# Seven products instead of eight for five heads' gate and value, four pairs instead of three in the MLP

## The chip, the cores and the metric

One core of a Trainium2 chip runs the whole program in one launch. The metric is the device time in microseconds of one execution, in the median of several; lower is better.

## The reference, cut to what matters

One layer of a trunk on 256 tokens of width 2048, in float32: a retention mixer with 8 heads, then a squared-ReLU MLP of width 8192, each behind an RMSNorm and added to its input, and a last RMSNorm.

```
h = rmsnorm(x, norm1)
q, k, v, g = split(h @ w_in, [2048, 4096, 8192])   # w_in 2048 x 12288; per head q,k 256, v,g 512 columns
q, k = rotary(q), rotary(k) * DK**-0.5
o = ((q @ k.T) * decay) @ v                         # chunk-causal, per head
o = head_norm(o) * silu(g)
x = x + o @ w_out                                   # 4096 x 2048
h = rmsnorm(x, norm2)
x = x + square(relu(h @ w_up)) @ w_down             # 2048 x 8192, 8192 x 2048
return rmsnorm(x, final_norm)
```

## The kernel before, in words

All weights are read once from HBM, 1 MB at a time, by DMAs that SyncE's queue issues in order. Every float32 operand is split in two float32r parts, a high one (a cast, on ScalarE) and a low one (operand minus high, on VectorE), and a product is three matmuls: high by high, high by low, low by high (lines 87 and 88, where the first two share one matmul of 512 columns, lines 102 to 106, and line 153). `load_block` loads a block of 128 x 2048 weights in `raw` (3 buffers) and splits it in two pairs `wh`, `wl` of 128 x 1024 (4 buffers of each); a buffer is free again once TensorE has read it for the last time.

The 128-row slices of the inner dimension are called kt; T = 256 tokens are NB = 2 row halves b. `proj_cols` makes queries and keys and the MLP's first product (weights stationary, tokens moving), `proj_rows` makes gates, values and the output product (tokens stationary, 512 weight columns moving): for each kt, each b and each 512 columns, three matmuls. A head h runs `gates`, `gate_silu`, `queries`, `values`; the rest of the previous head is put in between as fillers after a block: `mix(h-1)` in the gates, `turn(h-1)` (transposes of the result into `ys`) in the queries, `scores(h)` in the values.

The MLP's second product is done four times (q: 2048 of the 8192 rows), each in two halves of 1024 columns, by `seven`. Of the 16 kt of a q, the first 2*SP = 6 are three pairs; a pair of kt, the two row halves and the two column blocks are a 2 x 2 by 2 x 2 block product, done with seven block products instead of eight (Winograd's form of Strassen's scheme), 3 matmuls each and pair. The other 10 kt are done as in `proj_rows`, in 5 blocks (`regular`, r). Four weight blocks b11, b12, b22, b21 are loaded in `sraw`; four sums of them are made in place by VectorE (`plus`, line 196); the sums of the left side are made in `sums` beside the MLP's first product. Products that go to one quarter alone accumulate in its PSUM bank; those that go to several have banks of their own (`chain`, `fifth`) and are added to x by VectorE (`sub_out`, line 580). The order of r and of the seven products is a string: `"rwr13r25r6r74"`, where w is the loading of the four blocks; the last of the eight calls keeps 4 kt to the end (`late=4`) so that the quarters finish one after the other (`finish`).

Each engine works through its instructions in order. That order is set at build time by the Tile framework's list planner: of the instructions that are ready by its own costs it takes the one that is earliest in the program, so work written later can be put ahead of work that waits. All 8 PSUM banks are one rotating pool.

Of the kernel before, what the change touches and what calls it, by code (L numbers as in the profile page):

```python
# [28 lines left out]
SP = 3  # L29
QT = 16  # L30


@with_exitstack
def trunk_kernel(ctx: ExitStack, tc: tile.TileContext, io, out):

# [13 lines left out]
    def bank(name):  # L49
        return ps.tile([P, 512], F32, tag="bank", name=name)  # L50
# [28 lines left out]
    def proj_cols(src, xs, accs, fillers=()):  # L79
        for g in range(KT // 4):  # L80
            parts = load_block(src[g], 4, 512)
            for j, (wh, wl) in enumerate(parts):
                kt = 4 * g + j
                for o, acc in enumerate(accs):
                    c = slice(o * P, (o + 1) * P)
                    both = xs[:, kt].rearrange("p a t -> p (a t)")
                    nc.tensor.matmul(acc, wh[:, c], both, start=(kt == 0), stop=False)  # L87
                    nc.tensor.matmul(acc[:, :T], wl[:, c], xs[:, kt, 0, :], start=False, stop=(kt == KT - 1))  # L88
            for f in [f for at, f in fillers if at == g]:
                f()  # L90
# [3 lines left out]
    def proj_rows(blocks, per, xs, accs, nk, after=(), late=0, done=None, lead=None):  # L94
# [3 lines left out]
        def add(kt, wh, wl, b, cs):  # L98
            t = slice(b * P, (b + 1) * P)
            for c in cs:  # L100
                n = slice(c * 512, (c + 1) * 512)
                nc.tensor.matmul(accs[b][c], xs[:, kt, 0, t], wh[:, n], start=(kt == 0), stop=False)  # L102
                nc.tensor.matmul(accs[b][c], xs[:, kt, 0, t], wl[:, n], start=False, stop=False)  # L103
            for c in cs:
                n = slice(c * 512, (c + 1) * 512)
                nc.tensor.matmul(accs[b][c], xs[:, kt, 1, t], wh[:, n], start=False, stop=(kt == nk - 1))  # L106
# [19 lines left out]


    def seven(quads, blocks, xs, sx, sub_out, done, order, late=0):
        acc = [[bank("acc_d") for _ in range(2)] for _ in range(NB)]
        chain, fifth = bank("acc_s"), bank("acc_5")  # L130
        begun = set()
        raws = []

        def load():
            r = mp.tile([P, SP * 512], F32, tag="sraw", name="sraw", bufs=4)
            nc.sync.dma_start(r, quads[len(raws)])
            raws.append(r)
            return r

        def split(r):  # L140
            parts = []
            for p0 in range(0, SP, 2):
                n = min(2, SP - p0) * 512
# [12 lines left out]
        def product(to, key, r, left):  # L156
            parts = split(r)
            for p, (wh, wl) in enumerate(parts):
# [3 lines left out]
                mm(to, key, xl, wh, p == SP - 1)  # L162

        def part(k, b):
            return lambda p: (xs[:, 2 * p + k, 0, b * P : (b + 1) * P], xs[:, 2 * p + k, 1, b * P : (b + 1) * P])

        def total(i):
            return lambda p: (sx[:, p, i, 0], sx[:, p, i, 1])

        def add(kt, wh, wl, b, cs, last=False):  # L170
            t = slice(b * P, (b + 1) * P)
            for c in cs:
                n = slice(c * 512, (c + 1) * 512)
                mm(acc[b][c], (b, c), xs[:, kt, 0, t], wh[:, n], False)
                mm(acc[b][c], (b, c), xs[:, kt, 0, t], wl[:, n], False)
            for c in cs:
                n = slice(c * 512, (c + 1) * 512)
                mm(acc[b][c], (b, c), xs[:, kt, 1, t], wh[:, n], last)
# [3 lines left out]
        def regular(g):  # L182
            for j, (wh, wl) in enumerate(load_block(blocks[g], 2, 1024)):
                kt = 2 * SP + 2 * g + j
# [5 lines left out]

        def whole():
            for name in ("b11", "b12", "b22", "b21"):
                w[name] = load()

        def plus(to, other):
            nc.vector.tensor_add(w[to], w[to], w[other])

        def p1():
            product(chain, "s", w["b11"], total(0))
            sub_out(0, 0, chain, -1)  # L200

        def p2():
            product(acc[0][0], (0, 0), w["b21"], part(1, 0))

        def p3():
            product(acc[0][1], (0, 1), w["b22"], total(4))

        def p4():
            plus("b21", "b22")
            product(acc[1][0], (1, 0), w["b21"], part(1, 1))  # L210

        def p5():
            plus("b11", "b12")
            product(fifth, "5", w["b11"], total(1))
            sub_out(0, 1, fifth, 1)
            sub_out(1, 1, fifth, 1)
            plus("b12", "b22")

        def p6():
            plus("b22", "b11")  # L220
            product(chain, "s", w["b22"], total(2))
            sub_out(0, 1, chain, 1)

        def p7():
            product(chain, "s", w["b12"], total(3))
            sub_out(1, 0, chain, -1)
            sub_out(1, 1, chain, 1)

        w = {}
        steps = {"w": whole, "1": p1, "2": p2, "3": p3, "4": p4, "5": p5, "6": p6, "7": p7}  # L230
# [12 lines left out]


    xs = cp.tile([P, KT, 2, T], F32R, tag="xs", name="xs")
    xr = cp.tile([P, KT, T], F32, tag="ys", name="xr", padded_shape=[P, VT * 2, T])
# [13 lines left out]
    pw = bank("pw")  # L260
# [14 lines left out]
    with tc.tile_pool(name="ap", bufs=1) as ap:  # L275
# [32 lines left out]
        def first_norm():  # L308
# [6 lines left out]
            psr = bank("psr")  # L315
# [9 lines left out]
        def gates(h, after, lead=None):  # L325
            acc = [[bank("acc_g")] for _ in range(NB)]
            proj_rows(io["w_g"][h], 4, xs, acc, KT, after, lead=lead)
# [9 lines left out]
        def queries(h, fillers):  # L337
            acc = [bank("acc_qk") for _ in range(4)]
            proj_cols(io["w_qk"][h], xs, acc, fillers)
# [18 lines left out]
        def values(h, fillers):  # L358
            acc = [[bank("acc_v")] for _ in range(NB)]
            proj_rows(io["w_v"][h], 4, xs, acc, KT, fillers)  # L360
# [5 lines left out]
        def scores(h):  # L366

            qk = st["qk"]
            pst = bank("pst")
# [16 lines left out]
        def mix(h):  # L386
# [3 lines left out]
            for b in range(NB):  # L390
                po = bank("po")
# [20 lines left out]
        def turn(h):  # L412
            y = st["y"]
            for i in range(2):
                pt = bank("pt")
# [4 lines left out]
                for j in range(2):  # L420
                    k = 4 * h + 2 * i + j
                    split_scaled(ys[:, k], pt[:, j * T : (j + 1) * T], gain[:, k : k + 1])

        for h in range(H):
            if h == 0:
                gates(h, [], lead=lead_x)
                ys = cp.tile([P, VT, 2, T], F32R, tag="ys", name="ys")
# [5 lines left out]
                )  # L433
            else:
                gates(h, [(1, lambda h=h: mix(h - 1))])
                gate_silu()
                queries(h, [(1, lambda h=h: turn(h - 1))])
            if h == 0:
                nc.sync.dma_start(dec, io["dec"])
            values(h, [(1, lambda h=h: scores(h))])  # L440


        acc0 = [[bank("acc_o") for _ in range(2)] for _ in range(NB)]
# [5 lines left out]
    x1s = cp.tile([P, KT, 2, T], F32R, tag="xs", name="x1s")  # L449
# [26 lines left out]
    def turn_x(half):  # L476
        for i in range(4):
            pt = bank("ptx")
# [5 lines left out]
            for j in range(2):  # L484
                split_scaled(x1s[:, k0 + j], pt[:, j * T : (j + 1) * T], norm2[:, k0 + j : k0 + j + 1])
# [7 lines left out]
    acc1 = [[bank("acc_o") for _ in range(2)] for _ in range(NB)]  # L493
# [10 lines left out]
    def second_norm():  # L504
        psr = bank("psr2")
# [8 lines left out]
    big = cp.tile([P, VT * 2 * T], F32R, tag="ys", name="big")  # L514
    hs = big[:, : QT * 2 * T].rearrange("p (k a t) -> p k a t", k=QT, a=2)
    n0 = QT * 2 * T
    sx = big[:, n0 : n0 + SP * 5 * 2 * P].rearrange("p (k s a t) -> p k s a t", k=SP, s=5, a=2)
# [22 lines left out]
    def sums(p, s):  # L540


        a11, a21 = s[:, 0, :P], s[:, 0, P:]
        a12, a22 = s[:, 1, :P], s[:, 1, P:]
        u = mp.tile([P, 4, P], F32, tag="u", name="u")
        nc.vector.tensor_sub(u[:, 0], a21, a22)
        nc.vector.tensor_sub(u[:, 1], a11, u[:, 0])
        nc.vector.tensor_sub(u[:, 2], a21, a11)
        nc.vector.tensor_sub(u[:, 3], a12, u[:, 1])
        nc.scalar.copy(sx[:, p, 1:, 0], u)  # L550
        nc.vector.tensor_sub(sx[:, p, 1:, 1], u, sx[:, p, 1:, 0].bitcast(F32))
        for a in range(2):
            nc.scalar.activation(sx[:, p, 0, a], hs[:, 2 * p, a, :P].bitcast(F32), AF.Copy, scale=-1.0)

    for q in range(4):
        for c in range(4):
            acc = [bank("acc_u") for _ in range(4)]
            proj_cols(io["w_up"][4 * q + c], x1s, acc, [(1, second_norm)] if q == 0 and c == 0 else ())
            for i in range(2):
                s = mp.tile([P, 2, T], F32, tag="s", name="s", bufs=2)  # L560
                for j in range(2):
# [3 lines left out]
                    nc.scalar.copy(s[:, j], acc[o][:, T:])  # L565
                    nc.vector.tensor_add(s[:, j], acc[o][:, :T], s[:, j])
                    nc.vector.scalar_tensor_tensor(t, s[:, j], 0.0, rsrow2, op0=ALU.max, op1=ALU.mult)
                    nc.scalar.activation(s[:, j], t, AF.Square)
                    nc.scalar.copy(hs[:, k, 0], s[:, j])
                    nc.vector.tensor_sub(hs[:, k, 1], s[:, j], hs[:, k, 0].bitcast(F32))  # L570
                if 2 * c + i < SP:
                    sums(2 * c + i, s)
# [3 lines left out]
        for half in range(2):  # L576

            def sub_out(b, c, acc, sign, half=half):
# [5 lines left out]
                io["w_down_s"][q][half], io["w_down_r"][q][half], hs, sx, sub_out,  # L584
# [27 lines left out]

# [47 lines left out]
```

## Time and profile before

| | |
|---|---|
| median of 3 runs | 1473.11 us (1472.92 to 1474.33) |
| the profiled execution | 1472.67 us, its span 1470.5 us |
| TensorE matmul busy | 1453.9 us, 99% of the span, 7096 instructions |
| VectorE busy | 978.7 us, 67% |
| ScalarE busy | 735.3 us, 50% |
| GpSimd busy | 16.3 us, 1% |
| DMA | 280.45 MB, mean 191 GB/s |

The span is what lies between the first and the last instruction of the program in the trace; 2.2 us of the profiled execution lie around it. The duration that a row gives for a matmul is from issue to its modelled end; matmuls overlap, so what one costs is the distance between two starts.

### The profile page before, as it was taken

What the parts mean: (1) busy time and instruction counts of PE and PEld (TensorE: products, weight loads), DVE (VectorE), ACT (ScalarE), POOL (GpSimd) and SP (SyncE); (2) the same over time, 40 slices, a digit from 0 to 9 for tenths busy, and PEclk for the clock granted to TensorE, in tenths of its full rate; (3) what the DMA queues carried; (4) which work ended last, traced back from release to release, by engine and by line L of the source; (5) the groups of instructions that cost most, each with busy time, mean ns of one, the idle gap of its engine ahead of it and who ended that gap; (6) DMA issues with size and microseconds to landing.
All of it is one profiled execution on the core that took longest, in us unless ns stands there. A gap on an engine that the chain in (4) does not pass through costs nothing.

```text
span 1470.5 us, 18118 instructions
## 1 busy us (share of the span) xinstructions
PE 1453.9 (99%) x7096; PEld 1215.9 (83%) x7096; DVE 978.7 (67%) x1305; ACT 735.3 (50%) x994; POOL 16.3 (1%) x28
## 2 busy tenths in 40 slices
PE   9999999999999999999999999999999999999997
PEld 7788888888888888888888888888888888888885
DVE  6556565656565656546466689676897678866787
ACT  7444444444444444434345555465555555556554
POOL 0000000000000000000000000000000000000000
PEclk9999999999999999999999999999999999999999
DMA  9555555545555545765545545655556546565451
GB/s 349 210 186 181 174 175 191 176 172 174 191 177 175 176 174 194 268 239 180 197 170 177 198 153 185 240 197 175 177 187 234 179 165 209 192 215 186 172 200 58
DMA packets 43989, 280.45 MB, mean 191 GB/s; under 512 B 5248, under 2 KB 6144, under 8 KB 14208
## 3 DMA queue, kind: packets, MB, share of 16 engines
q1 hardware_dynamic: 43344, 276.15, 53.5%
q0 software_dynamic: 416, 3.15, 0.6%
q8 instruction: 55, 0.90, 0.2%
q14 instruction: 30, 0.25, 0.0%
q10 hardware_dynamic: 144, 0.01, 0.0%
HBM read 277.18 MB, written 2.10 MB: 190 GB/s over the span
## 4 chain that ended last, share of the span: by engine, by line
PE 96%; DVE 1%; ACT 1%; issue 1%; DMA 0%; POOL 0%; SPq 0%; POOLq 0%; ACTq 0%; DVEq 0%
PE acc_d L153 18%; PE acc_u L87 16%; PE acc_qk L87 8%; PE acc_u L88 8%; PE acc_qk L88 4%; PE acc_v L103 4%; PE acc_o L102 4%; PE acc_o L106 4%; PE acc_o L103 4%; PE acc_g L103 4%; PE acc_v L106 4%; PE acc_g L102 4%; PE acc_v L102 4%; PE acc_g L106 4%; PE acc_s L153 3%; PE po L397 1%
## 5 line engine op out<-in xcount | busy, mean ns | idle before, releaser
L65 DVE TENSOR_TENSOR wl<-raw,wh 128x1024 fp32r<-128x1024 f32 x456 | 553.4, 1223 | 429.1 <-ACT wh L64 428.6
L64 ACT CAST wh<-raw 128x1024 fp32r<-128x1024 f32 x456 | 475.2, 1049 | 520.1 <-PE acc_u L87 144.8
L87 PE MATMUL acc_u<-x1s,wh 128*128 128x512 f32 x1024 | 361.3, 397 | 0.0
L88 PE MATMUL acc_u<-x1s,wl 128*128 128x256 f32 x1024 | 286.4, 281 | 0.0
L153 PE MATMUL acc_d<-wh,big 128*128 128x512 f32 x784 | 245.2, 392 | 0.8 <-ACT wh L147 0.5
L87 PEld LDWEIGHTS acc_u<-x1s,wh 128*128 128x128 f32 x1024 | 192.3, 188 | 46.9
L88 PEld LDWEIGHTS acc_u<-x1s,wl 128*128 128x128 f32 x1024 | 191.8, 188 | 0.9 <-DVE wl L65 0.6
L87 PE MATMUL acc_qk<-xs,wh 128*128 128x512 f32 x512 | 181.8, 398 | 0.0
L153 PEld LDWEIGHTS acc_d<-wh,big 128*128 128x128 f32 x784 | 147.2, 188 | 33.9 <-ACT wh L147 0.9
L153 PE MATMUL acc_d<-wl,big 128*128 128x512 f32 x392 | 150.1, 393 | 0.0
L88 PE MATMUL acc_qk<-xs,wl 128*128 128x256 f32 x512 | 143.4, 281 | 0.0
L147 ACT CAST wh<-sraw 128x1024 fp32r<-128x1024 f32 x112 | 90.9, 834 | 104.2 <-PE acc_d L153 91.4
L87 PEld LDWEIGHTS acc_qk<-xs,wh 128*128 128x128 f32 x512 | 96.2, 188 | 23.3
L148 DVE TENSOR_TENSOR wl<-sraw,wh 128x1024 fp32r<-128x1024 f32 x112 | 103.3, 952 | 11.9 <-ACT wh L147 11.3
L103 PE MATMUL acc_v<-wl,xs 128*128 128x512 f32 x256 | 100.8, 394 | 0.7 <-DVE wl L65 0.7
L102 PE MATMUL acc_g<-wh,xs 128*128 128x512 f32 x256 | 100.3, 395 | 1.1 <-ACT wh L72 1.1
L103 PE MATMUL acc_g<-wl,xs 128*128 128x512 f32 x256 | 101.2, 395 | 0.0
L102 PE MATMUL acc_v<-wh,xs 128*128 128x512 f32 x256 | 100.3, 393 | 0.3 <-ACT wh L64 0.3
L102 PE MATMUL acc_o<-wh,ys 128*128 128x512 f32 x256 | 100.5, 392 | 0.0
L106 PE MATMUL acc_v<-wh,xs 128*128 128x512 f32 x256 | 100.1, 391 | 0.0
L103 PE MATMUL acc_o<-wl,ys 128*128 128x512 f32 x256 | 100.1, 391 | 0.0
L106 PE MATMUL acc_g<-wh,xs 128*128 128x512 f32 x256 | 99.7, 389 | 0.0
(114 smaller groups left out, 1507.2 us busy)
## 6 DMA issues: line engine op xcount, KB each, us to landing
raw<-in_w_up SPq DMA_DIRECT2D x64, 1024.0 KB, 4.9
raw<-in_w_down_r SPq DMA_DIRECT2D x40, 1024.0 KB, 4.9
raw<-in_w_qk SPq DMA_DIRECT2D x32, 1024.0 KB, 4.9
raw<-in_w_v SPq DMA_DIRECT2D x32, 1024.0 KB, 4.9
raw<-in_w_o SPq DMA_DIRECT2D x32, 1024.0 KB, 4.9
raw<-in_w_g SPq DMA_DIRECT2D x28, 1024.0 KB, 5.0
sraw<-in_w_down_s SPq DMA_DIRECT2D x32, 768.0 KB, 4.5
raw<-in_w_g SPq DMA_DIRECT2D x16, 256.0 KB, 6.6
```

What stands on the lines that cost most here:

```text
L64: nc.scalar.copy(wh, r)
L65: nc.vector.tensor_sub(wl, r, wh.bitcast(F32))
L87: nc.tensor.matmul(acc, wh[:, c], both, start=(kt == 0), stop=False)
L88: nc.tensor.matmul(acc[:, :T], wl[:, c], xs[:, kt, 0, :], start=False, stop=(kt == KT - 1))
L102: nc.tensor.matmul(accs[b][c], xs[:, kt, 0, t], wh[:, n], start=(kt == 0), stop=False)
L103: nc.tensor.matmul(accs[b][c], xs[:, kt, 0, t], wl[:, n], start=False, stop=False)
L106: nc.tensor.matmul(accs[b][c], xs[:, kt, 1, t], wh[:, n], start=False, stop=(kt == nk - 1))
L147: nc.scalar.copy(wh[:, :n], c)
L148: nc.vector.tensor_sub(wl[:, :n], c, wh[:, :n].bitcast(F32))
L153: nc.tensor.matmul(to, x, w, start=(key not in begun), stop=last, skip_group_check=True)
L397: nc.tensor.matmul(po, s, w, start=(n == 0), stop=(n == len(terms) - 1))
```

## The change

1. `seven` is made general: number of pairs from `sx`, weight buffers handed in (`raws`), the first result for a quarter of the output marked as first. Signs are moved to the left side, so that product 1 takes the plain high and low parts, without a negated copy (lines 552 and 553 go).
2. For heads 1 to 5, `gates`, `gate_silu` and `values` are replaced by `gates_values`: one product of 1024 columns (512 of g, 512 of v) by `seven` with SPR = 3 pairs and 5 regular blocks, order `"rwr1r3s2r56r74"` (s: the scores). Results go to two tiles in SBUF: ScalarE copies the first, VectorE adds the others. `mix(h-1)` and `turn(h-1)` move into the queries. The left sums are made once, in `sums_x`, in head 0's values. Heads 0, 6 and 7 stay as they were, with some fillers moved.
3. The MLP's second product takes SPM = 4 pairs and 4 regular blocks; order `"rw1r32r56r74"`, and `"rw1r3r25647r"` with `late=2` for the last call. Two of the four weight sums, b12 += b22 and b21 += b22, are made there by an accumulating DMA from SBUF to SBUF that GpSimd issues, 1 MB each; the other two stay on VectorE. In the program the sums stand directly behind the product that last needs the old block.
4. The 8 PSUM banks become two pools (sides) of 4. `ys`, `hs` and the raw weight blocks share three tiles of SBUF (ya, yb, yc).

```
-    def bank(name):
-        return ps.tile([P, 512], F32, tag="bank", name=name)
+    def bank(name, side):
+        return ps.tile([P, 512], F32, tag="bank%d" % side, name=name, bufs=4)
...
+        def plus(to, other):
+            if to in by_dma:
+                nc.gpsimd.dma_start(w[to], w[other], accum_op=ALU.add)
+            else:
+                nc.vector.tensor_add(w[to], w[to], w[other])
...
         def p1():
-            product(chain, "s", w["b11"], total(0))
-            sub_out(0, 0, chain, -1)
+            product(chain, "s", w["b11"], part(0, 0))
+            out(0, 0, chain, 1)
+            plus("b11", "b12")
+            plus("b12", "b22")
         def p2():
             product(acc[0][0], (0, 0), w["b21"], part(1, 0))
+            plus("b21", "b22")
         def p3():
-            product(acc[0][1], (0, 1), w["b22"], total(4))
+            product(acc[0][1], (0, 1), w["b22"], total(3))
+            plus("b22", "b11")
         def p4():
-            plus("b21", "b22")
             product(acc[1][0], (1, 0), w["b21"], part(1, 1))
...
+        def gates_values(h):
+            sg = ap.tile([P, NB, DV], F32, tag="sg", name="sg")
+            vf = ap.tile([P, NB, DV], F32, tag="xh", name="vf", bufs=2)
+            v = ap.tile([P, NB, 2, DV], F32R, tag="v", name="v")
+            to = (sg, vf)
+            def sub_out(b, c, bank, sign, first):
+                t = to[c][:, b]
+                if first:
+                    nc.scalar.copy(t, bank)
+                else:
+                    nc.vector.tensor_tensor(t, t, bank, op=ALU.add if sign > 0 else ALU.subtract)
+            def done(acc, b, c):
+                t = to[c][:, b]
+                nc.vector.tensor_add(t, t, acc[b][c])
+                if c == 0:
+                    nc.scalar.activation(t, t, AF.Silu, scale=rs[:, b : b + 1])
+                else:
+                    split_scaled(v[:, b], t, rs[:, b : b + 1])
+            seven(
+                io["w_gv_s"][i], io["w_gv_r"][i], [sraw[:, j] for j in range(4)], x0, st["sx"],
+                sub_out, done, "rwr1r3s2r56r74", 1, extra=lambda: scores(h),
+            )
...
+            elif h in STRASSEN_HEADS:
+                last = h == STRASSEN_HEADS[-1]
+                queries(h, [(1, lambda: mix(h - 1))] + ([] if last else [(3, lambda: turn(h - 1))]))
+                gates_values(h)
...
+                io["w_down_s"][q][half], io["w_down_r"][q][half], [raw3[:, j] for j in range(3)] + [raw1], hs, sx, sub_out,
...
-                "rw13r25r647rr" if last and half == 1 else "rwr13r25r6r74",
-                late=4 if last and half == 1 else 0,
+                "rw1r3r25647r" if last and half == 1 else "rw1r32r56r74",
+                1 - half, late=2 if last and half == 1 else 0, by_dma=("b12", "b21"),
```

## Rows read from the trace of the kernel before

**Rows 1.** The page, part 1: busy time of each engine.

```profile
PE 1453.9 (99%) x7096; PEld 1215.9 (83%) x7096; DVE 978.7 (67%) x1305; ACT 735.3 (50%) x994; POOL 16.3 (1%) x28
```

**Rows 2.** The page, part 4: the chain of waits by engine.

```profile
PE 96%; DVE 1%; ACT 1%; issue 1%; DMA 0%; POOL 0%; SPq 0%; POOLq 0%; ACTq 0%; DVEq 0%
```

**Rows 3.** Waits of whole span: who waited for whom, total, times, longest.

```profile
DVE wl L65 <- ACT wh L64: 428.6, 316, 3.6
ACT wh L64 <- PE acc_u L87: 144.8, 98, 2.9
```

**Rows 4.** Windows: head 1, its queries, the two halves of a second product.

```profile
core 0: us, PE busy (x) PEld busy (x) DVE busy (x) ACT busy (x) POOL busy (x), PEclk, DMA share, GB/s
79.76:150.62 70.86, 70.86 (x346) 59.46 (x345) 41.60 (x57) 32.53 (x40) 1.09 (x2) 1.00 0.51 177
103.84:127.32 23.48, 23.48 (x137) 20.50 (x136) 11.86 (x14) 11.64 (x17) 0.00 (x0) 1.00 0.52 183
1025.26:1067.41 42.15, 42.15 (x186) 34.30 (x185) 36.72 (x45) 24.12 (x34) 0.00 (x0) 1.00 0.50 173
1067.41:1109.56 42.15, 42.15 (x185) 34.21 (x184) 37.15 (x39) 21.51 (x25) 0.00 (x0) 1.00 0.57 199
```

**Rows 5.** Timeline of PE: start, duration, what; ends of two runs of matmuls.

```profile
127.32 0.39 PE L102 MATMUL acc_v<-wh,xs 128*128 128x512 f32 x1
...
138.31 0.81 PE L374 MATMUL pst<-qk 128*128 128x256 f32 x3
...
1025.26 0.39 PE L153 MATMUL acc_d<-wh,big 128*128 128x512 f32 x1
...
1109.56 0.39 PE L87 MATMUL acc_u<-x1s,wh 128*128 128x512 f32 x1
```

**Rows 6.** DVE by line and form in 1025.26 to 1109.56, busy and mean ns.

```profile
L65 DVE TENSOR_TENSOR wl<-raw,wh 128x1024 fp32r<-128x1024 f32 x18 | 21.5, 1221 | 5.5 <-ACT wh L64 5.5
L196 DVE TENSOR_TENSOR sraw<-sraw 128x1536 f32<-128x1536 f32 x8 | 14.1, 1758 | 0.2
L148 DVE TENSOR_TENSOR wl<-sraw,wh 128x512 fp32r<-128x512 f32 x14 | 9.6, 686 | 0.6 <-ACT wh L147 0.4
L580 DVE TENSOR_TENSOR x<-x,acc_s 128x512 f32<-128x512 f32 x8 | 5.3, 682 | 1.4 <-PE acc_s L153 1.4
L570 DVE TENSOR_TENSOR big<-s,big 128x256 fp32r<-128x256 f32 x4 | 1.6, 420 | 0.0
```

**Rows 7.** Timeline of DVE where head 2's queries end.

```profile
188.31 0.87 DVE L271 SCALAR_TENSOR_TENSOR ys<-pt,gain,ys 128x256 fp32r<-128x256 f32 x2
189.34 0.88 DVE L271 SCALAR_TENSOR_TENSOR ys<-pt,gain,ys 128x256 fp32r<-128x256 f32 x2 [0.15 <-ACT ys L270]
...
197.73 0.78 DVE L346 TENSOR_TENSOR sum<-acc_qk,sum 128x256 f32<-128x256 f32 x2
...
203.11 3.49 DVE L65 TENSOR_TENSOR wl<-raw,wh 128x1024 fp32r<-128x1024 f32 x3
```

**Rows 8.** DMA issues: form, count, KB each, median us to landing.

```profile
raw<-in_w_down_r SPq DMA_DIRECT2D x40, 1024.0 KB, 4.9
sraw<-in_w_down_s SPq DMA_DIRECT2D x32, 768.0 KB, 4.5
x<-in_x POOLq DMA_DIRECT2D x1, 2048.0 KB, 14.2
fnorm<-in_final_norm POOLq DMA_DIRECT2D x1, 1024.0 KB, 5.5
```

**Rows 9.** Timeline of DVE: the last quarter's add.

```profile
1461.43 0.68 DVE L456 TENSOR_TENSOR x<-acc_d,x 128x512 f32<-128x512 f32 x1
```

**Rows 10.** Timeline of PE: the last matmul.

```profile
1460.20 0.39 PE L153 MATMUL acc_d<-wh,big 128*128 128x512 f32 x1
```

More of the change, by code (lines that the diff above doesn't have):

```diff
@@ L28 @@
 WARM = 8
-SP = 3
+SPR = 3
+SPM = 4
 QT = 16
+STRASSEN_HEADS = range(1, 6)
 @with_exitstack
@@ L85, in proj_cols @@
                     c = slice(o * P, (o + 1) * P)
-                    both = xs[:, kt].rearrange("p a t -> p (a t)")
+                    both = xs[kt].rearrange("p a t -> p (a t)")
                     nc.tensor.matmul(acc, wh[:, c], both, start=(kt == 0), stop=False)
-                    nc.tensor.matmul(acc[:, :T], wl[:, c], xs[:, kt, 0, :], start=False, stop=(kt == KT - 1))
+                    nc.tensor.matmul(acc[:, :T], wl[:, c], xs[kt][:, 0, :], start=False, stop=(kt == KT - 1))
             for f in [f for at, f in fillers if at == g]:
@@ L124, in proj_rows, with seven @@
                     done(b, c)
-    def seven(quads, blocks, xs, sx, sub_out, done, order, late=0):
-        acc = [[bank("acc_d") for _ in range(2)] for _ in range(NB)]
-        chain, fifth = bank("acc_s"), bank("acc_5")
+    def seven(quads, blocks, raws, xs, sx, sub_out, done, order, side, late=0, extra=None, by_dma=()):
+        np_ = len(sx)
+        acc = [[bank("acc_d", side) for _ in range(2)] for _ in range(NB)]
+        fifth, chain = bank("acc_5", 1 - side), bank("acc_s", 1 - side)
         begun = set()
[L132 to L138, printed above, removed]
+        taken = set()
+        names = ("b11", "b12", "b22", "b21")
+        w = dict(zip(names, raws))
         def split(r):
             parts = []
-            for p0 in range(0, SP, 2):
-                n = min(2, SP - p0) * 512
+            for p0 in range(0, np_, 2):
+                n = min(2, np_ - p0) * 512
                 wh = wp.tile([P, 1024], F32R, tag="wh", name="wh", bufs=4)
@@ L156, in product @@
         def product(to, key, r, left):
-            parts = split(r)
-            for p, (wh, wl) in enumerate(parts):
+            for p, (wh, wl) in enumerate(split(r)):
                 xh, xl = left(p)
@@ L161, in product, with out @@
                 mm(to, key, xh, wl, False)
-                mm(to, key, xl, wh, p == SP - 1)
+                mm(to, key, xl, wh, p == np_ - 1)
         def part(k, b):
-            return lambda p: (xs[:, 2 * p + k, 0, b * P : (b + 1) * P], xs[:, 2 * p + k, 1, b * P : (b + 1) * P])
+            t = slice(b * P, (b + 1) * P)
+            return lambda p: (xs[2 * p + k][:, 0, t], xs[2 * p + k][:, 1, t])
         def total(i):
-            return lambda p: (sx[:, p, i, 0], sx[:, p, i, 1])
+            return lambda p: (sx[p][:, i, 0], sx[p][:, i, 1])
+        def out(b, c, acc, sign):
+            sub_out(b, c, acc, sign, (b, c) not in taken)
+            taken.add((b, c))
         def add(kt, wh, wl, b, cs, last=False):
@@ L189, in regular @@
                         add(kt, wh, wl, b, range(2), kt == QT - 1)
+        def plus(to, other):
[3 more added lines that the diff above has]
+                nc.vector.tensor_add(w[to], w[to], w[other])
         def whole():
[L192 to L196, printed above, removed]
+            for i, name in enumerate(names):
+                nc.sync.dma_start(w[name], quads[i])
         def p1():
-            product(chain, "s", w["b11"], total(0))
-            sub_out(0, 0, chain, -1)
+            product(chain, "s", w["b11"], part(0, 0))
+            out(0, 0, chain, 1)
+            plus("b11", "b12")
+            plus("b12", "b22")
         def p2():
             product(acc[0][0], (0, 0), w["b21"], part(1, 0))
+            plus("b21", "b22")
         def p3():
-            product(acc[0][1], (0, 1), w["b22"], total(4))
+            product(acc[0][1], (0, 1), w["b22"], total(3))
+            plus("b22", "b11")
         def p4():
-            plus("b21", "b22")
             product(acc[1][0], (1, 0), w["b21"], part(1, 1))
         def p5():
[L213 to L217, printed above, removed]
+            product(fifth, "5", w["b11"], total(0))
+            out(0, 1, fifth, 1)
+            out(1, 1, fifth, 1)
         def p6():
-            plus("b22", "b11")
-            product(chain, "s", w["b22"], total(2))
-            sub_out(0, 1, chain, 1)
+            product(chain, "s", w["b22"], total(1))
+            out(0, 1, chain, -1)
         def p7():
[L225 to L230, printed above, removed]
+            product(chain, "s", w["b12"], total(2))
+            out(1, 0, chain, 1)
+            out(1, 1, chain, -1)
+        steps = {"w": whole, "1": p1, "2": p2, "3": p3, "4": p4, "5": p5, "6": p6, "7": p7, "s": extra}
         g = 0
@@ L325, in gates @@
         def gates(h, after, lead=None):
-            acc = [[bank("acc_g")] for _ in range(NB)]
-            proj_rows(io["w_g"][h], 4, xs, acc, KT, after, lead=lead)
+            acc = [[bank("acc_g", 1)] for _ in range(NB)]
+            proj_rows(io["w_g"][h], 4, x0, acc, KT, after, lead=lead)
             st["acc_g"] = acc
@@ L421, in turn, with sums_x @@
                     k = 4 * h + 2 * i + j
-                    split_scaled(ys[:, k], pt[:, j * T : (j + 1) * T], gain[:, k : k + 1])
+                    split_scaled(ys[k], pt[:, j * T : (j + 1) * T], gain[:, k : k + 1])
+        def sums_x():
+            sx3 = ap.tile([P, 4, 2, P], F32R, tag="xh", name="sx3", bufs=2)
+            to = [sxc[:, 0], sxc[:, 1], sx3]
+            for p in range(SPR):
+                for k in (2 * p, 2 * p + 1):
+                    nc.scalar.activation(xr[:, k], xr[:, k], AF.Copy, scale=norm1[:, k : k + 1])
+                k = 2 * SPR + 2 * p
+                u = xr[:, k : k + 2].rearrange("p a (s t) -> p (a s) t", s=2)
+                sums(to[p], (xr[:, 2 * p], xr[:, 2 * p + 1]), u)
+            st["sx"] = to
+        def gates_values(h):
[16 more added lines that the diff above has]
+                    split_scaled(v[:, b], t, rs[:, b : b + 1])
+            i = h - STRASSEN_HEADS[0]
+            seven(
+                io["w_gv_s"][i], io["w_gv_r"][i], [sraw[:, j] for j in range(4)], x0, st["sx"],
+                sub_out, done, "rwr1r3s2r56r74", 1, extra=lambda: scores(h),
+            )
+            st["sg"], st["v"] = sg, v
         for h in range(H):
@@ L433, in trunk_kernel @@
                 )
-            else:
-                gates(h, [(1, lambda h=h: mix(h - 1))])
+                nc.sync.dma_start(dec, io["dec"])
+                values(h, [(1, sums_x), (2, lambda: scores(0))])
+                ys_part("ya", 0, 16)
+            elif h in STRASSEN_HEADS:
+                last = h == STRASSEN_HEADS[-1]
+                queries(h, [(1, lambda: mix(h - 1))] + ([] if last else [(3, lambda: turn(h - 1))]))
+                gates_values(h)
+                if last:
+                    ys_part("yb", 16, 12)
+                    ys_part("yc", 28, 4)
+            else:
+                first = h == STRASSEN_HEADS[-1] + 1
+                gates(h, ([(0, lambda: turn(h - 2))] if first else []) + [(2 if first else 1, lambda: mix(h - 1))])
                 gate_silu()
[L437 to L443, printed above, removed]
+                queries(h, [(1, lambda: turn(h - 1))])
+                values(h, [(1, lambda: scores(h))])
+        acc0 = [[bank("acc_o", 0) for _ in range(2)] for _ in range(NB)]
         proj_rows(io["w_o"][0], 2, ys, acc0, VT, [(1, lambda: mix(H - 1)), (4, lambda: turn(H - 1))])
@@ L492, in trunk_kernel @@
             add_residual(acc0, 0, b, c)
[L493 removed]
+    acc1 = [[bank("acc_o", 1) for _ in range(2)] for _ in range(NB)]
     proj_rows(io["w_o"][1], 2, ys, acc1, VT, [(2, lambda: turn_x(0))])
@@ L538, in finish @@
                 nc.sync.dma_start(out[b * P : (b + 1) * P, n], x[:, b, n])
[L540 to L553, printed above, removed]
     for q in range(4):
         for c in range(4):
-            acc = [bank("acc_u") for _ in range(4)]
+            acc = [bank("acc_u", (c + 1) % 2) for _ in range(4)]
             proj_cols(io["w_up"][4 * q + c], x1s, acc, [(1, second_norm)] if q == 0 and c == 0 else ())
             for i in range(2):
-                s = mp.tile([P, 2, T], F32, tag="s", name="s", bufs=2)
+                s = [mp.tile([P, T], F32, tag="s", name="s", bufs=4) for _ in range(2)]
                 for j in range(2):
@@ L564, in trunk_kernel @@
                     k = 4 * c + o
[L565 to L572, printed above, removed]
+                    nc.scalar.copy(s[j], acc[o][:, T:])
+                    nc.vector.tensor_add(s[j], acc[o][:, :T], s[j])
+                    nc.vector.scalar_tensor_tensor(t, s[j], 0.0, rsrow2, op0=ALU.max, op1=ALU.mult)
+                    nc.scalar.activation(s[j], t, AF.Square)
+                    nc.scalar.copy(hs[k][:, 0], s[j])
+                    nc.vector.tensor_sub(hs[k][:, 1], s[j], hs[k][:, 0].bitcast(F32))
+                if 2 * c + i < SPM:
+                    u = mp.tile([P, 4, P], F32, tag="u", name="u")
+                    sums(sx[2 * c + i], s, u)
         if q == 3:
@@ L576, in trunk_kernel, with sub_out @@
         for half in range(2):
-            def sub_out(b, c, acc, sign, half=half):
+            def sub_out(b, c, acc, sign, first, half=half):
                 n = slice(half * 1024 + c * 512, half * 1024 + (c + 1) * 512)
@@ L610, in _blocks, with _seven_blocks @@
     return np.ascontiguousarray(w).reshape(n // cols, k // (P * rows), P, rows * cols)
+def _seven_blocks(w, pairs):
+    lead = w.shape[:-2]
+    w = w.reshape(-1, QT, P, 1024)
+    s = w[:, : 2 * pairs].reshape(-1, pairs, 2, P, 2, 512).transpose(0, 2, 4, 3, 1, 5)
+    s = np.stack([s[:, i, j] for i, j in ((0, 0), (0, 1), (1, 1), (1, 0))], axis=1)
+    r = w[:, 2 * pairs :].reshape(-1, QT // 2 - pairs, 2, P, 1024).transpose(0, 1, 3, 2, 4)
+    return s.reshape(lead + (4, P, pairs * 512)), r.reshape(lead + (QT // 2 - pairs, P, 2048))
 def kernel(**inputs):
@@ L630, in cols @@
         return np.ascontiguousarray(u.reshape(n, P).T)
+    w_down = a["mlp_w_down"][0].reshape(4, QT * P, 2, 1024).transpose(0, 2, 1, 3)
+    w_down_s, w_down_r = _seven_blocks(w_down, SPM)
+    hs = slice(STRASSEN_HEADS[0], STRASSEN_HEADS[-1] + 1)
+    gv = np.concatenate([u.reshape(D, H, DV)[:, hs].transpose(1, 0, 2) for u in (g, v)], axis=2)
+    w_gv_s, w_gv_r = _seven_blocks(gv, SPR)
     arrays = {
```

79 lines of the change are left out of this document (46 added, 33 removed).

## The prediction, made before the change was run

> **What bounds the kernel now.** First the engines' busy shares: TensorE is busy 99% of the span, VectorE 67%, ScalarE 50% [rows 1]. Then the chain of waits, which says the same of the end: 96% of it is TensorE, and no DMA is in it [rows 2]. Then the waits: ScalarE's casts wait for TensorE to free a `wh` buffer, and VectorE's low parts wait for ScalarE [rows 3]; both are ahead of TensorE and held back by it. So each matmul taken away is worth its distance to the next, as long as VectorE keeps up. The windows show where that is in doubt: VectorE is busy 41.60 of 70.86 us in a head of the old kind, but 36.72 and 37.15 of 42.15 us (88%) in the two halves of a second product, with TensorE still without a gap there [rows 4]. The granted clock is 1.00 in all of them, the 2.4 GHz level, and I leave it there. The profiled execution took 1472.67 us, 0.44 under the median of the runs; I sum against the former and add the 0.44 at the end.
>
> **The price of a matmul** of 512 columns is the distance of starts. In head 1's values 48 matmuls lie between 127.32 and 138.31: 0.2290 us each. In the MLP 366 (two calls of 183) lie between 1025.26 and 1109.56: 0.2303 each [rows 5]. The difference, 0.0013 x 183 = 0.24 us per call, is all that the old `seven` loses to VectorE at 88%.
>
> **TensorE's part.** Gates and values of a head take 2 x 16 kt x 2 b x 3 = 192 matmuls now. By `seven`: 7 products x 3 pairs x 3 = 63, and 10 kt x 2 b x 2 c x 3 = 120, together 183: 9 fewer in each of five heads, 45. The MLP's call goes from 63 + 120 = 183 to 7 x 4 x 3 + 8 x 12 = 180: 3 fewer in eight calls, 24. That is 69 x 0.229 = 15.8 us less, 1456.9 us. The 10.3 us of it in the heads need VectorE to hold a new load there; the 5.5 in the MLP need the transfers to be on time.
>
> **VectorE in heads 1 to 5.** A 1024-column low part costs 3.49 / 3 = 1.16 us when several follow each other [rows 7], a 512-column one 0.69 and a weight sum of 1536 columns 1.76 [rows 6], about 0.08 less in a row. The stretch from the first r to the last product then holds 10 x 1.16 + 7 x (1.16 + 0.61) + 4 x 1.68 = 30.7 us; two `sub_out` and four adds of 0.6 (3.6; the first copy of each quarter goes to ScalarE, which is half idle); queries' sums and rotation, 203.11 - 197.73 = 5.4; turn's four, 1.75 [rows 7]; scores and the splits of v, some 2.6. Together 44.1, against 183 x 0.229 = 41.9 plus 2.0 for scores and transposes on TensorE, 43.9. As about 4 us (last adds, v) fall in the next queries, where VectorE has 11.86 of 23.48 us of work [rows 4] and gets some 3 us of mix as well, the stretch is 40 of 43.9, 91%: just above the 88% that cost 0.24 us.
>
> The tight place is its start. Let t = 0 be the first r matmul; three `wl` buffers are then ready, as now. VectorE does rotation and turn from -1.25 (0.46 us before the queries end plus 0.79 us of transposes) to 5.9, the second r's last part to 7.1, product 1's two to 8.8, then the two sums that the program puts ahead of the third r, b11 and b12, to 12.2, the third r's first part to 13.3. TensorE gets there after 48 matmuls of r and 9 of product 1, at 13.05, and its second matmul, the first that reads the low part, is due at 13.3. So it fits with nothing to spare; afterwards VectorE gains. If the rotation ended later, up to the 3.4 us of the two sums would show. Bounds 0 and 3.4 us per head; I take the 0.24 of the like stretch, 1.2 us in all.
>
> **The MLP's transfers.** Per call VectorE's own sums go from 4 x 1.68 to 2 x 2.26 (1.76 x 2048/1536, less 0.08), its product splits from 7 x 1.77 to 14 x 1.16, its regular splits from 10 x 1.16 to 8 x 1.16: 0.7 us less than before, so its load is no worry. What is new is a wait: b22 += b11 on VectorE may start only when the transfer b12 += b22 has read b22. Queued behind it on VectorE stand low parts of product 2, and TensorE waits for those. Again with t = 0 at the first r: the last evictions of the first product (12 instructions of 0.42 in three lines like L570's [rows 6]) and product 1's second part end at 4.7, b11 += b12 at 6.9; the transfer starts then. TensorE is at product 2's second half after 78 matmuls, 17.86; ahead of that stand the sum (2.26) and a split (1.16), so the transfer must land by 14.4, 7.5 us after its start. The second transfer, b21 += b22, has 19 us (two r and three products) before product 4 and is hidden; in the last call it has only three products, 8.2 us.
>
> No row shows an accumulating transfer. From below: 1 MB by the same queue, GpSimd's, landed in 5.5 us. From above: 2 MB by that queue, under load, in 14.2. The loads give a slope of (4.9 - 4.5) per 256 KB, 1.6 us per MB [rows 8]; if the target has to be read too, 5.5 + 1.6 = 7.1, the nearest that the rows give for one in quiet, and with a load running beside it more. I take 8.0, 0.5 us late, in the seven calls of the common order: 3.5 us. Ends: 0, and 6.7 x 7 = 47.
>
> The Trainium skill ("Collectives: The Full Stack", section on the bandwidth ceiling) bears on this from the other side: an add in the DMA engine needs two source reads on one ring and ran there at half the rate of a copy (ratio 1.93). No row here shows that. By it the 1 MB's own part of the landing would double; an estimate from that page and the load's 4.9 us is 9.8 us (twice 4.9), and the sum would go up by some 13 us, towards the rival of late transfers below.
>
> **What I cost at nothing.** `sums_x` (six scalings on ScalarE, three sets of four short subtractions and one split, 5 us of VectorE) lies in head 0's values, where VectorE has as much room as in other heads; uncovered it is 5 us once. Loads: the bytes are the same, 16 MB of transfers come on top of 280 and the DMA share in the second product is 0.50 to 0.57 [rows 4]; SyncE's queue waits for buffers, not for HBM. The banks: with two sides of four the queries' first four banks need `chain` free, which product 7's two results release while product 4 runs (9 x 0.229 = 2.06 us, the reads 0.68 each [rows 6]); turn's two banks go straight to the quarters, and the planner can put the other row half's matmuls first. Bounds 0 and 1 us per call. The tail: keeping 2 kt instead of 4 spaces the last quarters by 6 x 0.229 = 1.37 instead of 2.75 us. The last add starts now 1461.43 - 1460.43 = 1.0 us after the last matmul is through [rows 9, 10], as it stands behind another quarter's; it could be 2.4. I take no change.
>
> **Sum.** 1472.67 - 15.8 + 1.2 + 3.5 = 1461.6; on the median 1462.
>
> **The rivals.**
> (a) VectorE becomes the bound in the heads. For: 44.1 us of work in a stretch of 43.9, with the two early sums ahead of a split that is due. Against: the old second halves run gapless at 88%, and the planner can move work. Taking 2.2 us in each head, the middle of 1 and 3.4: 11 instead of 1.2, 1472; the heads would gain nothing.
> (b) The transfers land late, the slower side. Place: the eight calls of `seven`, VectorE's queue in front of b22 += b11. Price: (landing - 7.5) in seven calls. It takes back all that was gained from a landing of 9.6 us on (15.8 - 1.2 = 14.6 over seven calls gives 2.1), and is slower by over 3 us from 10.0 on. At 11.5 us: 28 us, 1486. For: a target that must be read, loads in the same engines, and a planner that may put the sum too early in VectorE's queue. Against: 5.5 us for a plain megabyte, and the planner may as well put product 2's parts ahead of the sum, which lengthens the cover to the next r, another 1.4 us.
> (c) The change doesn't do what it says: the split of the banks makes TensorE wait where eight rotating ones did not, some 0.7 us in each of 13 calls, 9 us: 1471.
>
> **How the numbers follow.** The forecast 0.66 (1456 to 1467), (a) 0.12, (b) 0.17, (c) 0.05. Against 1473.1, 0.2% or 3 us is about what a measurement of this kernel can tell from no change. Faster: the forecast and nearly all of (a) and (c) in their lower parts, 0.76; within 3 us: 0.07; slower: (b), 0.17. The low end is the bare matmul count with no new stall, 1456; the high end takes in (a), (c) and of (b) landings up to 10.4 us, 1479.
>
> **What would show it.** 69 fewer matmuls of 512 columns from heads and second product. The distance of starts stays 0.229 to 0.231 in the heads' new stretches and in the MLP's (right), or goes over 0.235 there (a, b). A wait of VectorE's L-line of the weight sums for a DMA, with low parts and then TensorE late behind it, would show (b); in the transfer rows a landing under 8 us would exclude it. Waits of TensorE for reads of banks would show (c). The forecast is wrong if TensorE's gaps in these stretches come to more than 10 us, or if VectorE's work there is above 95% of the time.

## The result and the profile after

The changed kernel takes 1481.34 us (median of 4 runs, 1480.31 to 1482.88), the kernel before 1473.65 on the same chip: ratio 1.0053, 95% interval 1.0036 to 1.0071. It is 0.5% slower, where 1462 was forecast and 1479 was the upper end; rival (b), the late transfers, is what happened.

The page's parts 1 and 4 of the changed kernel, against [rows 1, 2]: TensorE has 69 matmuls less and is busy 4.9 us less, but in a span that is 10.6 us longer; VectorE's share of the chain went from 1 to 5%, a DMA's from 0 to 4%.

```profile
PE 1449.0 (98%) x7027; PEld 1208.2 (82%) x7027; DVE 1056.0 (71%) x1398; ACT 778.2 (53%) x1027; POOL 29.2 (2%) x44
...
PE 88%; DVE 5%; DMA 4%; issue 2%; ACT 1%; SPq 0%; POOLq 0%; POOL 0%; ACTq 0%; DVEq 0%
```

Windows of it (columns as in [rows 4]): head 1, then head 1's seven products alone, then first and second half of the first second product.

```profile
82.14:151.01 68.87, 68.87 (x338) 57.69 (x336) 53.38 (x71) 36.95 (x50) 1.10 (x2) 1.00 0.48 168
...
107.59:151.01 43.42, 43.42 (x195) 35.57 (x193) 38.05 (x50) 24.77 (x35) 0.00 (x0) 1.00 0.47 159
...
841.87:883.41 41.54, 41.54 (x182) 33.75 (x181) 36.74 (x42) 26.09 (x32) 1.75 (x2) 1.00 0.73 226
883.41:931.73 48.32, 43.34 (x182) 34.97 (x181) 36.18 (x35) 23.10 (x22) 1.71 (x2) 0.96 0.70 218
```

The heads did as was forecast: 68.87 us instead of 70.86 [rows 4], no gap, VectorE at 88% of the stretch. So did this first half: 41.54 us (those of the other three q take 41.6 to 42.6). The second half lost almost 7 us, at a lower granted clock. Among the waits of the whole span (who waited for whom, total, times, longest), these lines are new. L204 is the line of `plus` that VectorE does, L153 the low parts of `split`, L158 the matmuls of `seven`:

```profile
DVE raw L204 <- DMA raw<-raw: 24.2, 8, 6.3
...
PEld acc_d L158 <- DVE wl L153: 17.5, 9, 5.4
...
PE acc_d L158 <- DVE wl L153: 13.9, 6, 5.0
```

What happens there is read from four timelines around 891 to 911 us: GpSimd's queue, SyncE's, VectorE, TensorE.

```profile
891.43 0.86 POOL L202 DMA_DIRECT2D raw<-raw  x1 [30.35 <-DVE raw L204]
```

```profile
892.06 17.21 SPq L63 DMA_DIRECT2D raw<-in_w_up  x2
```

```profile
903.22 2.29 DVE L204 TENSOR_TENSOR raw<-raw 128x2048 f32<-128x2048 f32 x1 [6.32 <-DMA raw<-raw]
905.43 1.22 DVE L153 TENSOR_TENSOR wl<-raw,wh 128x1024 fp32r<-128x1024 f32 x1
```

```profile
901.11 0.62 PE L158 MATMUL acc_d<-wh,hs 128*128 128x512 f32 x2
906.70 0.80 PE L158 MATMUL acc_d<-wl,hs 128*128 128x512 f32 x1 [4.97 <-DVE wl L153]
907.29 1.06 PE L158 MATMUL acc_d<-wh,hs 128*128 128x512 f32 x2
```

The transfer b12 += b22 is issued at 891.43. A load of 1 MB follows it at 892.06 (the row merges two loads; the second came 17 us later), and the sum b22 += b11 starts only at 903.22, after 6.32 us of waiting. Behind it stands product 2's second low part, and TensorE stands still for 4.97 us for that. Then its matmuls come 0.43 us apart instead of 0.23: the granted clock of 906.70 to 910.20 is 0.51, the 1.2 GHz level.

```profile
906.70:910.20 3.50, 3.50 (x8) 2.84 (x9) 3.35 (x3) 0.96 (x1) 0.85 (x1) 0.51 0.56 112
```

The DMA view of three windows tells why. First a first half's transfer (846 to 858 us), behind which a load starts 2.4 us later, then the one at 891, then the last call's (1432 to 1443), which has no load beside it; kind of queue (q0 is GpSimd's, q1 SyncE's): packets, MB, share of the engines' time, then the landings (time from issue to arrival).

```profile
q0 software_dynamic: 144, 1.05, 49.3%
q1 hardware_dynamic: 122, 1.00, 20.6%
...
raw<-raw POOLq DMA_DIRECT2D x1, 1024.0 KB, 8.0
```

```profile
raw<-raw POOLq DMA_DIRECT2D x1, 1024.0 KB, 11.7
raw<-in_w_up SPq DMA_DIRECT2D x1, 1024.0 KB, 11.2
```

```profile
q0 software_dynamic: 144, 1.05, 47.1%
q1 hardware_dynamic: 3, 0.00, 0.0%
...
raw<-raw POOLq DMA_DIRECT2D x1, 1024.0 KB, 7.0
```

Alone a transfer lands in 7.0 us. With a load that starts 0.6 us behind it, both take over 11 us here; in the other two second halves with such a load the transfers land in 9.9 and 10.5 us, the loads in 9.5 and 10.0. For a megabyte, a transfer keeps the DMA engines busy 2.3 times as long as a load does (49.3% for 1.05 MB against 20.6% for 1.00, both of the same 12 us); the transfer that is alone (47.1% of 11 us) keeps them busy 2.0 times as long as that load. The Trainium skill ("Collectives: The Full Stack", section on the bandwidth ceiling) gives 1.93 as the ratio of a copy's rate to that of an add with two source reads, there for collectives; the trace's 2.0 agrees. The prediction's estimate of 9.8 us from that page is not what a transfer alone takes, 7.0.

### The profile page after: what moved, and what is told of

Its sections match the earlier page's. It is cut to its first block, busy times and chain, and to the rows that moved or that the text cites. A ratio compares the mean times of both kernels' runs of the same rounds, so it can differ in the third digit from the quotient of the medians.

```text
span 1481.1 us, 18172 instructions
## 1 busy us (share of the span) xinstructions
PE 1449.0 (98%) x7027; PEld 1208.2 (82%) x7027; DVE 1056.0 (71%) x1398; ACT 778.2 (53%) x1027; POOL 29.2 (2%) x44
## 4 chain that ended last, share of the span: by engine, by line
PE 88%; DVE 5%; DMA 4%; issue 2%; ACT 1%; SPq 0%; POOLq 0%; POOL 0%; ACTq 0%; DVEq 0%
PE acc_d L158 21%; PE acc_u L93 16%; PE acc_u L94 8%; PE acc_qk L93 8%; PE acc_s L158 5%; PE acc_qk L94 4%; PE acc_o L108 4%; PE acc_o L112 4%; PE acc_o L109 4%; DMA raw<-raw 4%; PE acc L158 2%; DVE wl L153 1%; PE acc_v L109 1%; PE acc_v L112 1%; PE acc_v L108 1%
## 5 line engine op out<-in xcount | busy, mean ns | idle before, releaser
L71 DVE TENSOR_TENSOR wl<-raw,wh 128x1024 fp32r<-128x1024 f32 x410 | 497.7, 1222 | 299.9 <-ACT wh L70 298.8
L70 ACT CAST wh<-raw 128x1024 fp32r<-128x1024 f32 x410 | 428.9, 1051 | 426.5 <-PE acc_u L93 140.7
L158 PE MATMUL acc_d<-wh,hs 128*128 128x512 f32 x640 | 208.8, 400 | 0.0
L152 ACT CAST wh<-raw 128x1024 fp32r<-128x1024 f32 x112 | 117.2, 1049 | 122.7 <-PE acc_d L158 105.0
L153 DVE TENSOR_TENSOR wl<-raw,wh 128x1024 fp32r<-128x1024 f32 x112 | 134.6, 1221 | 41.5 <-ACT wh L152 40.7
L158 PE MATMUL acc_d<-wh,xs 128*128 128x512 f32 x460 | 147.7, 394 | 0.0
L158 PEld LDWEIGHTS acc_d<-wh,hs 128*128 128x128 f32 x640 | 123.5, 193 | 27.0
L158 PE MATMUL acc_d<-wl,hs 128*128 128x512 f32 x320 | 128.8, 404 | 14.9 <-DVE wl L153 13.9
L158 PEld LDWEIGHTS acc_d<-wh,xs 128*128 128x128 f32 x460 | 86.4, 188 | 19.4 <-issue 0.7
L94 PEld LDWEIGHTS acc_qk<-xs,wl 128*128 128x128 f32 x512 | 96.0, 188 | 1.7 <-DVE wl L71 0.8
L158 PE MATMUL acc_d<-wl,xs 128*128 128x512 f32 x230 | 90.0, 391 | 0.0
L158 PEld LDWEIGHTS acc_d<-wl,hs 128*128 128x128 f32 x320 | 61.9, 194 | 32.7 <-DVE wl L153 17.5
L153 DVE TENSOR_TENSOR wl<-sraw,wh 128x1024 fp32r<-128x1024 f32 x70 | 65.5, 953 | 15.0 <-ACT wh L152 14.9
L204 DVE TENSOR_TENSOR raw<-raw 128x2048 f32<-128x2048 f32 x16 | 36.6, 2288 | 24.2 <-DMA raw<-raw 24.2
```

The costliest lines, as they stand in the source:

```text
L70: nc.scalar.copy(wh, r)
L71: nc.vector.tensor_sub(wl, r, wh.bitcast(F32))
L94: nc.tensor.matmul(acc[:, :T], wl[:, c], xs[kt][:, 0, :], start=False, stop=(kt == KT - 1))
L158: nc.tensor.matmul(to, x, w, start=(key not in begun), stop=last, skip_group_check=True)
```

## The experiments

The theory: the transfers of the second halves land late because a load shares the DMA engines, VectorE's queue stands behind them, and TensorE's stall and the clock's fall after it cost all that is lost. (A stall is the distance between two matmul starts less 0.23 us.) The rivals: VectorE's load with four pairs; the split of the banks and the early sums; something else that slows the transfers. The first four ran beside a kernel before of 1473.94 us, the others beside one of 1473.11. "Pair" is the time of the two calls of one q.

**Heads alone.**

```
-SPM = 4
+SPM = 3
-                "rw1r3r25647r" if last and half == 1 else "rw1r32r56r74",
-                1 - half, late=2 if last and half == 1 else 0, by_dma=("b12", "b21"),
+                "rw13r25r647rr" if last and half == 1 else "rwr13r25r6r74",
+                1 - half, late=4 if last and half == 1 else 0,
```

> The heads' part alone: the MLP's second product goes back to three pairs, its old order and all four weight sums on VectorE. Theory (late transfers in the MLP's calls cost all that is lost): the MLP stage takes what it took in the kernel before (620 us from its first second product to the end), the heads keep their 8.7 us, so 1465 us, ratio to before 0.994. Rival (the split of the banks or the early sums cost time wherever seven products are used): the MLP stage stays several us longer than before, 1470 or more.

1466.63 us, ratio 0.9951 (0.9939 to 0.9964): the heads' part is a gain of 7.3 us. The pairs take 84.6 to 84.7 us against 84.29, so banks and new `seven` cost them 0.3 to 0.4 us; the last call has one stall of 2.1 us for a low part with a slow stretch behind it. The theory's total is met within 1.6 us, but not its number for the MLP stage: in the profiled execution, the slowest of the five (1468.98), that takes 624.1 us instead of 620.0. Of these 4.1 us, 3.1 are the last pair's. So the rival has a share of about 1 us in three pairs, and whether the other executions have the stall is not shown.

**No transfer.**

```
-                ..., by_dma=("b12", "b21"),
+                ...,
```

> The whole change with all four sums on VectorE, no transfer. Theory: the waits for transfers and the clock's falls go (about 24 us), but VectorE, busy 73 of 89 us in a pair of calls, gets 9 us more, 82 against 82.5 us of matmuls: it is full and gives part of it back, so 1462 to 1472 us. Rival (VectorE's load with four pairs is what bounds these calls, transfers or not): 1481 or slower.

1467.30 us, ratio 0.9955 (0.9942 to 0.9967): 14 us faster than the change with transfers, though VectorE does two sums more per call. A pair takes 85.2 us. What is left in it is one wait of TensorE per first half (the third row; the rows above it are VectorE's, the second early sum and the low parts behind it).

```profile
847.39 2.29 DVE L204 TENSOR_TENSOR raw<-raw 128x2048 f32<-128x2048 f32 x1
...
850.52 2.35 DVE L71 TENSOR_TENSOR wl<-raw,wh 128x1024 fp32r<-128x1024 f32 x2
```

```profile
851.80 0.73 PE L158 MATMUL acc_d<-wl,hs 128*128 128x512 f32 x2 [1.67 <-DVE wl L71]
```

**Only b21's sum by transfer.** `by_dma=("b21",)`, nothing else.

> The whole change with b12 += b22 back on VectorE; only b21 += b22, which nothing on VectorE stands behind, is a transfer. Theory: VectorE never waits for a transfer in front of low parts; a pair of calls takes 83 to 84.5 us instead of 89 to 91, so 1459 to 1463 us, ratio to before 0.991. Rival (VectorE's load): a pair of calls stays at 88 us or more, 1478 or slower, as VectorE gets 2.3 us more per call.

1467.92 us, ratio 0.9960 (0.9947 to 0.9974). VectorE waits for no transfer any more, and the kernel is 13 us faster than the changed one. But a pair takes 84.9 us, not 83 to 84.5: with b12 += b22 back on VectorE the same 1.67 us as without transfers appear, and the forecast of 1459 to 1463 is missed by 5. I had missed the early sums.

**Both transfers, more cover.**

```
         def p2():
             product(acc[0][0], (0, 0), w["b21"], part(1, 0))
-            plus("b21", "b22")
         def p3():
             product(acc[0][1], (0, 1), w["b22"], total(3))
             plus("b22", "b11")
+            plus("b21", "b22")
...
-                "rw1r3r25647r" if last and half == 1 else "rw1r32r56r74",
+                "rw1r3r25647r" if last and half == 1 else "rw1r2r3r5674",
```

(The last call, whose order is unchanged, keeps b21's sum behind product 2.)

> Both transfers stay, but product 2 and one regular block more stand between the first transfer and the sum that waits for it (order r w 1 r 2 r 3 r 5 6 7 4, b21's sum behind product 3), in seven of the eight calls. Theory: the sum finds its transfer landed (18 us of cover against landings of 7 to 12), no stall, no fall of the clock: a pair of calls 83 to 86 us, 1460 to 1466 us (the four products in a row at the end may press VectorE). Rival (VectorE's load, the same here): no better than the changed kernel, 1478 or slower.

1468.80 us, ratio 0.9964 (0.9951 to 0.9976). VectorE's waits for transfers fall from 24.2 to 3.4 us. The expected 1460 to 1466 is missed by 3: products 6 and 7 in a row use one bank, and TensorE waits for its reads in seven calls, 6.4 us in all:

```profile
PE acc_s L158 <- DVE x L650: 6.4, 7, 1.2
```

**More cover, and an r between products 6 and 7.** As before, but `"rw1r2r356r74"`.

> Both transfers, more cover for the first (r 1 r 2 r 3), and an r between products 6 and 7, which share a bank (order r w 1 r 2 r 3 5 6 r 7 4). Theory: the 0.9 us that TensorE waited for that bank in each call of the first cover run goes, a pair of calls takes 83 to 84 us, 1459 to 1463 us; then transfers are harmless once covered. Rival (they cost by themselves, as they share the DMA engines with loads): loads come late somewhere, 1467 or more.

1461.26 us, ratio 0.9918 (0.9905 to 0.9932); a pair takes 82.93 us, 0.2304 a matmul. Second halves still have landings of 10.2 to 11.8 us, which stop TensorE nowhere in the pairs. So in these pairs a transfer that has enough cover costs nothing (82.93 us here, 82.98 without any, below); the kernel with both of them, in another order, is 20 us faster than the change. The last call keeps its order and its stalls.

**No transfer, late sums.** Each sum of the MLP stands ahead of the product that needs it:

```
         def p5():
+            if "s" not in order:
+                plus("b11", "b12")
             product(fifth, "5", w["b11"], total(0))
...
+            if "s" not in order:
+                plus("b12", "b22")
         def p6():
+            if "s" not in order:
+                plus("b22", "b11")
             product(chain, "s", w["b22"], total(1))
```

(b21's ahead of product 4; the early ones in products 1 to 3 are left to the heads, whose order has an s.)

> No transfer, and in the MLP each of the four sums stands directly ahead of the product that needs it (as in the kernel before) instead of behind the product that last used the old block. Theory (what is left with all sums on VectorE is a low part queued behind the two early sums, 1.7 us at the third r of each first half): that wait goes, a pair of calls takes 83.3 to 84.2 us instead of 85.2, total 1461 to 1463. Rival (VectorE is simply full at four pairs): the wait turns up elsewhere, 1466 or more.

1460.69 us, ratio 0.9911 (0.9897 to 0.9924): the best, 1.4% under the change and 0.9% under the kernel before. TensorE has no gap in the pairs (82.98 us), though VectorE is busy for 97 to 99% of their halves:

```profile
839.81:881.30 41.49, 41.49 (x182) 33.83 (x181) 40.87 (x44) 26.12 (x32) 0.00 (x0) 1.00 0.50 175
881.30:922.79 41.49, 41.49 (x181) 33.82 (x180) 40.32 (x37) 23.15 (x22) 0.00 (x0) 1.00 0.58 202
```

That refutes VectorE's load as the cause: it is higher here than in the changed kernel, and costs nothing.

**Late sums, b21's by transfer.** As the last, with `by_dma=("b21",)` and that sum behind b22 += b11.

> As the run with late sums, and b21 += b22 by transfer, issued behind b22 += b11, with product 6, an r and product 7 (11 us) as cover. Theory: landings of 7 to 12 us are barely covered, so it is no better than without transfers: 1461 to 1466, ScalarE's cast of b21 waits for the transfer by up to 3 us in second halves. Rival (VectorE is full and 2.3 us less per call help): 1458 or less.

1462.37 us, ratio 0.9927 (0.9915 to 0.9940); a pair takes the same 82.98 us, its landings being 9.9 to 11.5. No gain from relieving VectorE, as expected; its interval overlaps the one without transfers, though every execution here took longer than every one there. The last call is where it loses: its order has no r and no product 7 between that transfer and product 4, ScalarE's cast waits 5.5 us for the landing (7.0 us), and TensorE stalls for 2.4 and 1.0 us, with a slow stretch behind them.

**The load behind the transfer.** The changed kernel with its order; the next first product's first block, in the three second halves that have one, comes by GpSimd's queue.

```
-            nc.sync.dma_start(raw, src)
+            (queue or nc.sync).dma_start(raw, src)
...
-            proj_cols(..., [(1, second_norm)] if q == 0 and c == 0 else ())
+            proj_cols(..., [(1, second_norm)] if q == 0 and c == 0 else (), nc.gpsimd if q and c == 0 else None)
```

> The changed kernel, but the one load that is issued 0.6 us after the first transfer of the second halves (the next first product's first block) goes through GpSimd's queue behind that transfer, in the three calls that have one. Theory (the landing of 10 to 12 us there comes from the two sharing the DMA engines): the first transfers of all second halves land in 7 to 8.5 us, VectorE's wait there falls from 4.5 to 6.3 us to 1 to 3, and the kernel takes 1466 to 1473 us. Rival (something else in the second halves slows the transfer): landings stay at 10 to 12 us and the time at 1481.

1467.65 us, ratio 0.9958 (0.9944 to 0.9971). The first transfers of these halves land in 7.9 to 8.0 us instead of 9.9 to 11.7; VectorE's waits there are 2.6 to 2.9 us instead of 4.5 to 6.3. Its GpSimd queue and VectorE at the place shown above, and the landing of the first transfer:

```profile
891.33 0.85 POOL L202 DMA_DIRECT2D raw<-raw  x1 [30.37 <-DVE raw L204]
892.24 0.56 POOL L63 DMA_DIRECT2D raw<-in_w_up  x1
```

```profile
899.38 2.29 DVE L204 TENSOR_TENSOR raw<-raw 128x2048 f32<-128x2048 f32 x1 [2.58 <-DMA raw<-raw]
```

```profile
raw<-raw POOLq DMA_DIRECT2D x1, 1024.0 KB, 8.0
```

The same bytes move at the same place, only in one row behind each other, and 13.7 us come back: TensorE's stalls there shrink to 1.4 to 1.7 us, and no slow stretch follows them. That shows the cause of these 13.7 us: the load beside the transfer. 6.4 us still lie between this kernel and the better order above, and most of that is cover: with landings of 7.9 to 9.3 us, first transfers still stall TensorE for 1.2 to 1.7 us in three second halves and one first half, 5.7 us in all. The run with more cover does not have these stalls.

## Why the prediction was wrong

**Matmuls and heads: right.** 69 fewer; a head is 1.99 us shorter (2.06 by count), 10.0 us in five, where 10.3 - 1.2 was forecast. VectorE's part of the stretch was put at 91% and is 88%. The tight start, and rival (a) with it, did not show. Rival (c) is out: the changed kernel's waits have no line of TensorE waiting for a bank's reader, and what banks and new `seven` cost together is 0.3 to 0.4 us per pair in the run of the heads alone.

**The deadline in the MLP: right.** The sum had to start 14.4 us after a call's first matmul. In the first half it started at 856.49 - 841.87 = 14.6, and TensorE lost nothing; in the third q's first half, after a landing of 9.0 us, at 15.6, and TensorE lost 1.0. In the second halves it started at 19.8, 18.0 and 18.6 us: 5.4, 3.6 and 4.2 late, and TensorE's stalls, the distance of starts less 0.23, were 5.1, 3.4 and 3.9 us. VectorE's queue was in the order that I had assumed. The second transfer was not hidden everywhere: in the last call "only three products, 8.2 us" were set against the landing alone (7.0), without the cast and the low part that come between it and product 4. There ScalarE waited 2.9 us for the landing, and TensorE stalled for 0.7 and 0.9 us.

**The landing: the step that failed.** I took 8.0 us, "0.5 us late, in the seven calls of the common order: 3.5 us". The figure holds for the first halves (8.0 to 9.0), and 7.1 for one in quiet was 7.0. It fails where it was carried to all calls. In three second halves a load starts 0.6 us behind the transfer (in first halves 2.4 us), and landings are 9.9 to 11.7. The text named this ("with a load running beside it more") and did not look in SyncE's queue for where it would be. Also the transfer starts later there, 891.43 - 883.41 = 8.0 us after the call's first matmul instead of the 6.9 worked out from the first half, so the cover was 6.4 us, not 7.5. In place of 3.5 us over seven calls, TensorE's stalls for first transfers came to 12.4 us in three second halves alone. Rival (b) named the place and the wait; its price, landing less 7.5 in seven calls, is not how the time came about.

**The clock: not in the sum at all.** The prediction left the granted clock at 1.00. After each of the three long stalls 8 to 13 matmuls come about 0.43 us apart, which costs 7.0 us in all. The stalls of all calls are 16.0 us, of which the kernel before has 1.1 too; so stalls and clock are 22 of the 24.7 us by which the MLP stage missed its bare count (from the first second product to the end 639.2 us, against 620.0 - 5.5 = 614.5). Another 1.4 are the tail, below; 1.4 are left over, spread over the pairs. Price (b) should have carried a slow stretch behind each of its long stalls.

**The tail: outside what I took.** I left it as it was, with 2.4 us named as the late end. The last matmul starts 11.7 us before the end, 10.3 before the change [rows 10]: 1.4 us, most of it that end. The last add now starts 1471.81 - 1469.65 = 2.2 us after the last matmul is through (its start at 1469.42 plus 0.23), against 1.0 [rows 9]:

```profile
1471.81 0.68 DVE L536 TENSOR_TENSOR x<-acc_d,x 128x512 f32<-128x512 f32 x1
```

The profiled execution (1482.88) has 2.4 us more up to the end of head 0's values, part of it a fall of the clock there that seven of the ten profiles of this study do not show.

## What to carry to other kernels

A transfer that replaces work of a busy engine must land before what is queued behind its reader is due; work out that due time call by call, and look up in the load queue what else starts beside it, since a landing time is one of its neighbours as much as its own. Where the cover is short, order is the cheapest cure: a product and a block moved between issue and reader, or the sums put right ahead of their use, turned 0.5% slower into 0.8 to 0.9% faster. An engine that is 97% busy need not be the bound: VectorE was that busy in the run with late sums, and TensorE had no gap.

## What I had not expected

A transfer and a load that start together both pay: alone 7.0 us, a load 4.9, together 9.9 to 11.7 and 9.5 to 11.2. And each single stall of 3.4 to 5.1 us, in a stretch that is otherwise full, is followed by 3.4 to 5.6 us at the 1.2 GHz level. So is the one of 2.1 us in the run of the heads alone, while those of 1.2 to 1.8 us in the load-behind and the no-transfer runs are followed by none.
